# Hybrid decoder block on one core: sums on DVE alone, a ninth weight slot and an earlier spare tile, logits in one step, down bias moved

## The chip, the core and the metric

The kernel runs on one core of a Trainium2 chip. Its engines are PE (TensorE), DVE (VectorE), ACT (ScalarE), POOL (GpSimd) and SP (SyncE), which here only issues DMAs. The time is that of the device, in microseconds, for one execution.

## The reference

One layer for 256 tokens of width 1024, all in float32: a modulated norm, four token mixers that share one input projection, a gated merge, an output projection, and then a mixture of 32 experts of which each token uses four.

```python
mod = c_act @ w_ada[l] + b_ada[l]
shift1, scale1, gate1, shift2, scale2, gate2 = (m[:, None, :] for m in jnp.split(mod, 6, axis=-1))
h = rms_norm(x, g_norm_mix[l]) * (1.0 + scale1) + shift1
z = h @ w_in[l]                      # four mixers' inputs and the merge logits
...
up = jnp.einsum('bsnc,ncd->bsnd', ys, w_branch[l])
gates = jax.nn.sigmoid(merge_logits.reshape(B, S, N_BRANCHES, D))
x = x + gate1 * (jnp.sum(gates * up, axis=2) @ w_out[l])
h2 = rms_norm(x, g_norm_ffn[l]) * (1.0 + scale2) + shift2
# moe_ffn: logits = h2 @ w_router + b_router; top 4 of 32; softmax over them
for e in range(N_EXPERTS):
    gu = h @ w_gate_up[e] + b_gate_up[e]
    ...
    y = y + combine[:, e:e + 1] * (act @ w_down[e] + b_down[e])
return rms_norm(x + gate2 * y, g_final)
```

The weights of the experts are 192 tiles of 2 MiB (four `wg` and two `wd` for each expert), 403 MB; all of the kernel reads 468 MB.

## The kernel before

**Products in float32.** Each large product of the front is made from two halves of both operands: `split` (L335) lets ACT write the rounded high half (L347) and DVE the rest, source minus high half (L348), and PE then does three products (high by high, high by low, low by high). The split works on 512 columns at a time, in four rotating buffers each.

**The front, 0 to 307 us.** The six vectors of the modulation are sums over 8 blocks of rows of `w_ada`, each row block scaled by the conditioning. For four of them `ada` (L237) does this in halves of 512 columns, step by step in the background of other work: the first four blocks are scaled by ACT (L249; for one vector by POOL, L247) and added by POOL (L251), the other four scaled and added by DVE (L254); `ada_end` lets PE transpose and reduces the sum. The mixers' projections and the merge use `z_unit` (L364): four splits of 512, each followed by 12 matmuls and a step of the background work (`bg`, the mixers; `slow_step`, the sums). A merge unit, 16 in all (four branches by four column blocks), is one `z_unit`, a sigmoid on ACT, the branch's up-projection `pu` (L809, from two splits of 256), a multiplication by the gate on DVE (L816) and an addition into `mix`, on POOL for the second and third branch (L817). The output projection `pw` (L765) runs in the last branch's units; `out_split` (L768) first lets POOL multiply each 512 columns of `wo` by `gate1` (L774).

**The router, 307 to 320 us.** `x1_logits` transposes the new x and multiplies it with the router's weights in four strips of 32 rows, a copy of the result (L895) and a second product with a selecting matrix (L896) add the strips. DVE finds the top four, their mask and positions. The gather `pg` (L1000) picks the expert's tokens by a matmul with a 0/1 matrix `pm`.

**The experts.** 16 pairs. For a pair PE does gate-up (`ea`, `eb`, L1067; its bias is a small matmul, L1058), a transposition (`eat`, L1081) and down (`ed`, L1094) of the one expert and then of the other; `spread` (L1032) prepares from the combine weights, with products by POOL (L1024), the matrices by which `scatter` (`py`, L1104) adds the pair's rows to the tokens. `down_bias` (L959) adds the bias of the down projections of all experts at once: two transposes, four matmuls `pyb` (L970), eight DVE operations.

**What sets the order.** A scheduler places each engine's instructions by the program's order and dependences; `tc.issue_after` holds an instruction behind another. Expert tiles go through a ring: `load_wide` (L134) takes the next slot and issues the load on SP, whose queue works in order, so that a load that waits for its slot holds all that follow. There are 5 slots (`RING`, used as 1 MiB halves in the front) and 3 more (`EXTRA`) from the third merge branch on, when the mixers' buffers are closed. Eight tiles are loaded into them during the output projection. A spare tile (`sp`, the first expert's fourth) uses space that the front gives back. In the program the bias rows `bgu` (L953, four loads on SP) stand ahead of it, in a buffer that is free after the router's mask.

## Time and profile before

| | |
|---|---|
| median of 3 runs | 1263.29 us (1259.78 to 1267.72) |
| profiled execution | 1264.25 us, span 1262.5 us |
| PE busy | 1172.2 us (93%) |
| DVE busy | 484.4 us (38%) |
| ACT busy | 204.8 us (16%) |
| POOL busy | 131.2 us (10%) |
| read from HBM | 467.81 MB |
| mean granted clock | 0.991 |

The shares are means over stages with different limits. The chain of waits says what released the last work at each step; the windows show which engine is full in a stage and at which rate the DMA runs; the waits of SP show when a load stood for its slot, and the waits of PE when PE stood for a load. A busy PE is not PE at its peak, since the ends of matmuls are modelled.

### The profile page before, as it was taken

What the parts mean: (1) busy time and instruction counts of PE and PEld (TensorE: products, weight loads), DVE (VectorE), ACT (ScalarE), POOL (GpSimd) and SP (SyncE); (2) the same over time, 40 slices, a digit from 0 to 9 for tenths busy, and PEclk for the clock granted to TensorE, in tenths of its full rate; (3) what the DMA queues carried; (4) which work ended last, traced back from release to release, by engine and by line L of the source; (5) the groups of instructions that cost most, each with busy time, mean ns of one, the idle gap of its engine ahead of it and who ended that gap; (6) DMA issues with size and microseconds to landing.
All of it is one profiled execution on the core that took longest, in us unless ns stands there. A gap on an engine that the chain in (4) does not pass through costs nothing.

```text
span 1262.5 us, 14878 instructions
## 1 busy us (share of the span) xinstructions
PE 1172.2 (93%) x6204; PEld 567.7 (45%) x6204; DVE 484.4 (38%) x833; ACT 204.8 (16%) x403; POOL 131.2 (10%) x171
## 2 busy tenths in 40 slices
PE   7999999989999999999999999999989998989875
PEld 4778798987333433333333333333323332332224
DVE  3797598986342312222222223222212222132123
ACT  3458355445100000000000000000000000000001
POOL 2332213740000000000000000000000000000001
PEclk9999899999999999999999999999999999999999
DMA  9975369947889999999999999999999999999994
GB/s 324 337 248 201 133 221 341 346 160 276 320 365 396 429 427 429 427 427 428 428 428 428 428 428 428 426 428 427 429 427 428 427 428 428 428 427 428 427 382 145
DMA packets 74730, 469.88 MB, mean 372 GB/s; under 512 B 6425, under 2 KB 27010, under 8 KB 50594
## 3 DMA queue, kind: packets, MB, share of 16 engines
q1 hardware_dynamic: 74034, 467.64, 90.6%
q10 hardware_dynamic: 624, 1.23, 0.3%
q8 instruction: 50, 0.82, 0.3%
q14 instruction: 22, 0.18, 0.0%
HBM read 467.81 MB, written 1.05 MB: 371 GB/s over the span
## 4 chain that ended last, share of the span: by engine, by line
PE 61%; DMA 23%; DVE 10%; issue 2%; ACT 1%; POOL 1%; ACTq 0%; SPq 0%; POOLq 0%; DVEq 0%
DMA wd<-in_w_down_dram 13%; PE ed L1094 13%; PE ea L1067 12%; PE eb L1067 12%; DMA wg<-in_w_gate_up_dram 9%; PE pz_m L361 5%; PE py L1104 4%; PE pg L1000 2%; PE pw L765 2%; PE pu L809 1%; PE pdl L1128 1%; DMA wada<-in_w_ada_dram 1%; PE eat L1081 1%; DVE el L1045 1%; DVE el L1047 1%
## 5 line engine op out<-in xcount | busy, mean ns | idle before, releaser
L1067 PE MATMUL ea<-wg,he 128*64 128x512 f32 x1024 | 284.9, 600 | 8.9 <-DMA wg<-in_w_gate_up_dram 8.7
L1067 PE MATMUL eb<-wg,he 128*64 128x512 f32 x1024 | 283.6, 593 | 0.0
L1094 PE MATMUL ed<-wd,aT 128*64 128x512 f32 x960 | 214.6, 598 | 9.5 <-DMA wd<-in_w_down_dram 8.3
L1041 DVE TENSOR_SCALAR eg<-ea 128x512 f32<-128x512 f32 x32 | 22.1, 692 | 356.6 <-PE ea L1067 352.5
L1043 ACT ACTIVATE es<-eg 128x512 f32<-128x512 f32 x32 | 20.2, 630 | 827.9 <-DVE eg L1041 827.9
L1067 PEld LDWEIGHTS eb<-wg,he 128*64 128x64 f32 x1024 | 80.2, 137 | 146.9 <-issue 146.8
L1067 PEld LDWEIGHTS ea<-wg,he 128*64 128x64 f32 x1024 | 72.9, 137 | 145.6 <-issue 119.4
L1094 PEld LDWEIGHTS ed<-wd,aT 128*64 128x64 f32 x960 | 67.4, 137 | 143.8 <-issue 126.9
L1024 POOL TENSOR_TENSOR pc<-pm,comb 128x128 f32<-128x128 f32 x64 | 23.5, 402 | 685.2 <-PE psm L1032 624.3
L361 PE MATMUL pz_m<-hh,wl_m 128*128 128x256 f32 x256 | 73.3, 286 | 5.9 <-DVE wl_m L348 5.8
L361 PE MATMUL pz_m<-hh,wh_m 128*128 128x256 f32 x256 | 73.6, 287 | 0.0
L361 PE MATMUL pz_m<-hl,wh_m 128*128 128x256 f32 x256 | 72.1, 282 | 0.0
L1106 DVE TENSOR_TENSOR x_sb<-x_sb,py 128x512 f32<-128x512 f32 x60 | 41.3, 688 | 30.3 <-PE py L1104 30.3
L361 PEld LDWEIGHTS pz_m<-hh,wl_m 128*128 128x128 f32 x256 | 49.0, 191 | 8.0 <-DVE wl_m L348 7.7
L1104 PE MATMUL py<-oa,sm 128*128 128x512 f32 x60 | 33.8, 645 | 19.4 <-DVE oa L1098 19.4
L361 PEld LDWEIGHTS pz_m<-hl,wh_m 128*128 128x128 f32 x256 | 49.1, 192 | 0.1
L361 PEld LDWEIGHTS pz_m<-hh,wh_m 128*128 128x128 f32 x256 | 49.0, 191 | 0.3
L1097 DVE TENSOR_TENSOR oa<-ed,late 64x512 f32<-64x512 f32 x15 | 10.2, 683 | 94.6 <-PE ed L1094 94.6
L1097 DVE TENSOR_TENSOR ob<-ed,late 64x512 f32<-64x512 f32 x15 | 10.2, 682 | 91.0 <-PE ed L1094 91.0
L348 DVE TENSOR_TENSOR wl_m<-win_m,wh_m 128x512 fp32r<-128x512 f32 x44 | 42.0, 971 | 7.0 <-ACT wh_m L347 6.9
L1058 PE MATMUL ea<-bgu,ident 32*64 32x512 f32 x128 | 36.5, 612 | 0.0
L1081 PEld LDWEIGHTS eat<-ident,el 128*128 128x128 f32 x128 | 17.6, 205 | 41.0 <-DVE el L1047 39.3
(450 smaller groups left out, 1567.8 us busy)
## 6 DMA issues: line engine op xcount, KB each, us to landing
wg<-in_w_gate_up_dram SPq DMA_DIRECT2D x128, 2048.0 KB, 26.7
wd<-in_w_down_dram SPq DMA_DIRECT2D x60, 2048.0 KB, 27.0
wada<-in_w_ada_dram SPq DMA_DIRECT2D x13, 1024.0 KB, 7.4
win_m<-in_w_in_dram SPq DMA_DIRECT2D x11, 1024.0 KB
win_c<-in_w_in_dram SPq DMA_DIRECT2D x8, 1024.0 KB, 8.2
wada<-in_w_ada_dram SPq DMA_DIRECT2D x12, 512.0 KB, 7.3
wl<-in_w_down_dram SPq DMA_DIRECT2D x5, 1024.0 KB, 28.8
wada<-in_w_in_dram SPq DMA_DIRECT2D x4, 1024.0 KB, 8.1
```

The lines of the kernel that those rows point to most:

```text
L348: V.tensor_tensor(lk, sk, f32(wk), ALU.subtract)
L361: T.matmul(pz[:, b * 256:(b + 1) * 256], l, r, start=(kh == 0 and b == 0 and kk == 0 and i == 0), stop=last and i == 2, skip_group_check=True)
L765: T.matmul(pw[t, hf_], m_[:, kk, t * P:(t + 1) * P], w[:, 0, :], start=(k == 0 and i == 0), stop=(k == KC - 1 and i == 2))
L1000: last_i["pg"] = T.matmul(pg[:, kk * 256:(kk + 1) * 256], chan(n2[:, t, :], k), pm[:, t].rearrange("p e s -> p (e s)"), start=(i == 0), st ...
L1024: G.tensor_tensor(pc[:, t, :, var, i ^ var, :], pv_[:, :, i, :], cv[:, :, i].unsqueeze(2).to_broadcast([P, EB // 2, CAP]), ALU.mult)
L1041: V.tensor_scalar(g, pa, 7.0, None, ALU.min)
L1058: T.matmul(pp_[64 * j:64 * j + 64, :], ident[r:r + NE, r + e:r + e + 1].to_broadcast([NE, CAP]), bgu[r:r + NE, :], start=True, stop=False, ...
L1067: T.matmul(pp_[64 * j:64 * j + 64, :], he[:, k, (e % EB) * CAP:(e % EB + 1) * CAP], w[:, i * DE + j * 512:i * DE + (j + 1) * 512], start=F ...
L1081: T.transpose(pt[:, q * P:(q + 1) * P], cols, ident)
L1094: T.matmul(pd[64 * jj:64 * jj + 64, :], aT[:, k % 4, 64 * (k // 4):64 * (k // 4) + 64], w[k % 4][:, o * 512:(o + 1) * 512], start=(k == 0) ...
L1104: T.matmul(py, s_[:, hf_, t * P:(t + 1) * P], o, start=True, stop=True)
L1106: V.tensor_tensor(yv, yv, py, ALU.add)
```

## The change

Seven things, in the order of the program.

1. The sums of the modulation (`ada`) are done for all 1024 columns at once by DVE alone, eight operations per vector; ACT and POOL no longer take part.
2. `split` works on 1024 columns: a `z_unit` does two splits instead of four, a branch unit one of 512 instead of two of 256, a row block of `wo` one instead of two. There are three rotating buffers of 1024 instead of four of 512.
3. The small subtraction L403 and the additions into `mix` are DVE's. `wo` is no longer multiplied by `gate1`; instead `out_last` multiplies each finished 512 columns of the projection by it before x is added.
4. The router's product gives the logits of 128 tokens directly, in eight accumulating matmuls; the copies and the selecting product go. The chain after it runs per token tile.
5. `bgu` is loaded on ACT's queue into a buffer of its own when the mixers close. Behind the eight tiles SP so finds the spare tile, which now waits for the last multiplication of the projection, and then a ninth tile, in a slot that joins the ring there.
6. `spread` and the first pair's `scatter` come after the gate-up of expert 2.
7. `down_bias` is done in four quarters behind the scatters of experts 8, 10, 12 and 14.

The core of the diff:

```diff
-WP = 4
+WP = 3
...
-    def ada(s_, j):
...
+    def ada(s_, i):
+        w = load_rows(f"wada{s_}_{i}", w_ada[0, i * 512:(i + 1) * 512, s_ * D:(s_ + 1) * D], D)
...
         def run():
-            for k in range(4):
-                if s_ == 2:
-                    G.tensor_tensor(w[k], w[k], cact[:, k:k + 1].to_broadcast([P, 512]), ALU.mult)
+            for kk in range(4):
+                k = 4 * i + kk
+                if k == 0:
+                    V.tensor_scalar(acc, w[kk], cact[:, k:k + 1], None, ALU.mult)
                 else:
-                    A.activation(w[k], w[k], AF.Copy, scale=cact[:, k:k + 1])
-                if k:
-                    G.tensor_tensor(w[0], w[0], w[k], ALU.add)
+                    V.scalar_tensor_tensor(acc, w[kk], cact[:, k:k + 1], acc, ALU.mult, ALU.add)
                 yield
-            for k in range(4, KC):
-                V.scalar_tensor_tensor(acc, w[k], cact[:, k:k + 1], w[0] if k == 4 else acc, ALU.mult, ALU.add)
-                yield
...
-        for k in range(nk if sw else 1):
-            wk, lk, sk = [t[:, k] for t in (wh, wl, src)] if sw else (wh, wl, src)
-            A.activation(wk, sk, AF.Copy)
-            V.tensor_tensor(lk, sk, f32(wk), ALU.subtract)
-        return ws
+            A.activation(wh, src, AF.Copy)
+            V.tensor_tensor(wl, src, f32(wh), ALU.subtract)
+        return wh, wl
...
     def z_unit(tiles, c0, name, token, sw=False):
         pz = bank("z", f"pz_{name}")
-        for kh in range(4):
-            wh, wl = split(tiles[kh // 2][:, 2 * (kh % 2):2 * (kh % 2) + 2, c0:c0 + 256], 2, 256, f"{name}_{kh}", sw)
-            z_part(pz, wh, wl, kh, token)
-            bg()
-            slow_step()
+        for i in range(2):
+            wh, wl = split(tiles[i][:, :, c0:c0 + 256], 4, 256, f"{name}_{i}", sw)
+            for j in range(2):
+                z_part(pz, wh[:, 2 * j:2 * j + 2, :], wl[:, 2 * j:2 * j + 2, :], 2 * i + j, token)
+                bg()
+                slow_step()
...
-            (G if kk else V).tensor_tensor(hl[:, k, :], hf, f32(hh[:, k, :]), ALU.subtract)
+            V.tensor_tensor(hl[:, k, :], hf, f32(hh[:, k, :]), ALU.subtract)
...
-            for w in (wo[k], wo[k + 1]):
-                for h in range(2):
-                    c = slice(h * 512, (h + 1) * 512)
-                    G.tensor_tensor(w[:, c], w[:, c], gate1[:, c], ALU.mult)
...
+            bgu = lb.tile([P, 512], F32, tag="bgu", name="bgu")
+            for j in range(4):
+                A.dma_start(bgu[NE * j:NE * j + NE, :], b_gate_up[0, :, j * 512:(j + 1) * 512])
...
-                (V if bi == 3 else G).tensor_tensor(mv, mv, sg, ALU.add)
+                V.tensor_tensor(mv, mv, sg, ALU.add)
...
-        V.tensor_tensor(x_sb[:, t, cs], x_sb[:, t, cs], pw[t, g], ALU.add)
+        tm = mp.tile([P, 512], F32, tag="t2", name=f"gx{t}{g}")
+        V.tensor_tensor(tm, pw[t, g], gate1[:, cs], ALU.mult)
+        V.tensor_tensor(x_sb[:, t, cs], x_sb[:, t, cs], tm, ALU.add)
...
-            T.matmul(pls[t][32 * kk:32 * kk + 32, 0:P], wr2[:, 4 * g + kk, :], xt[:, kk, :], start=(g == 0),
-                     stop=(g == 1))
...
+            pl_i[t] = T.matmul(pls[t][:, 0:NE], xt[:, kk, :], wr2[:, k, :], start=(k == 0), stop=(k == KC - 1)).ins
...
-        V.tensor_copy(lT[:, t, :], pls[t][:, 0:P])
-        sel_i = T.matmul(pls[t][:, P:P + NE], lT[:, t, :], id4, start=True, stop=True, skip_group_check=True).ins
...
+    add_slots(ctx.enter_context(tc.tile_pool(name="r9", bufs=1, side="right")), 1)
     with tc.tile_pool(name="sp", bufs=1, side="right") as sp:
         u = wg_src(0, 3)
         pref[u[0]] = load_wide(*u, pool=sp)
-        gate_up_bias(0, (sel_i, sel_i))
+        u = units[RING + EXTRA]
+        pref[u[0]] = load_wide(*u)
+        gate_up_bias(0, (pl_i[1], pl_i[1]))
...
             a0 = gate_up(e, he)
+            if late_sc:
+                sm = spread(b, pm)
+                scatter(0, sm[0], *late_sc.pop())
...
-                down_bias()
-            if sm is None:
+            elif sm is None:
                 sm = spread(b, pm)
             down(e + 1, a1, oa, ob)
+            if e == 0:
+                late_sc.append((oa, ob))
+                continue
             scatter(e, sm[r], oa, ob)
+            if 8 <= e < 16:
+                down_bias(e // 2 - 4)
```

What this does to the order on the engines, at three places.

SP's queue behind the first tiles, before (`wg_3_3563` is a tile of the second expert, `wd_0_3565` the eighth tile, `wg_3_3710` the spare):

```order
L136 DMA wg_3_3563<-in_w_gate_up_dram 128x4096
L136 DMA wd_0_3565<-in_w_down_dram 128x4096
L953 DMA bgu<-in_b_gate_up_dram 32x512 x4
L136 DMA wg_3_3710<-in_w_gate_up_dram 128x4096
L136 DMA wd_1_3889<-in_w_down_dram 128x4096
L136 DMA wd_0_3969<-in_w_down_dram 128x4096
```

and now (`wg_3_3310` is the spare, `wd_1_3312` the tile in the ninth slot):

```order
L134 DMA wg_3_3166<-in_w_gate_up_dram 128x4096
L134 DMA wd_0_3168<-in_w_down_dram 128x4096
L134 DMA wg_3_3310<-in_w_gate_up_dram 128x4096
L134 DMA wd_1_3312<-in_w_down_dram 128x4096
L134 DMA wd_0_3522<-in_w_down_dram 128x4096
L134 DMA wd_1_3532<-in_w_down_dram 128x4096
```

The four bias loads have left the queue; the spare and the ninth tile follow the eighth, and the load `wd_0_3522` is the first behind them that waits for a slot that an expert used.

PE at the router, before (`pnt` are the transposes of x, `pl` the router's products, `pb` the rows of the last gate, `ppos` the positions from the mask):

```order
L865 MATMUL pnt_3619<-ident,x_sb 128x128 x4
L865 MATMUL pnt_3631<-ident,x_sb 128x128 x4
L873 MATMUL pl_3528<-x1T_3624,wr_1632 32x128 x4
L873 MATMUL pl_3529<-x1T_3636,wr_1632 32x128 x4
L896 MATMUL pl_3528<-sel 128x32
L896 MATMUL pl_3529<-sel 128x32
L294 MATMUL pb_0_3653<-ident,modT 128x128 x4
L294 MATMUL pb_1_3654<-ident,modT 128x128 x4
L911 LDWEIGHTS ustr
L911 MATMUL ppos<-mask,ustr 128x32
L912 LDWEIGHTS oneb
L912 MATMUL ppos<-mask,oneb 128x32
```

and now:

```order
L857 MATMUL pnt_3239<-ident,x_sb 128x128
L867 MATMUL pl_3144<-wr_1514,scr 128x32 x4
L857 MATMUL pnt_3239<-ident,x_sb 128x128 x3
L912 LDWEIGHTS ustr
L912 MATMUL ppos<-mask,ustr 128x32
L913 LDWEIGHTS oneb
L913 MATMUL ppos<-mask,oneb 128x32
L867 MATMUL pl_3144<-wr_1514,scr 128x32 x4
L289 MATMUL pb_0_3252<-ident,modT 128x128 x4
L289 MATMUL pb_1_3253<-ident,modT 128x128 x4
L914 LDWEIGHTS ustr
L914 MATMUL ppos<-mask,ustr 128x32
```

The two selecting products are gone; the first token tile's `ppos` stands ahead of the second's last products.

PE at the first two experts' down projections, before (`ed_3880` of the first expert stands ahead of this piece; `ed_3968` is the second's):

```order
L963 MATMUL pct<-ident,comb 32x128 x2
L1094 MATMUL ed_3968<-wd_0_3969,aT_3876 64x512
L970 MATMUL pyb_3925<-bdn,cT 128x512
L970 MATMUL pyb_3930<-bdn,cT 128x512
L970 MATMUL pyb_3935<-bdn,cT 128x512
L1094 MATMUL ed_3968<-wd_0_3969,aT_3876 64x512 x2
L970 MATMUL pyb_3940<-bdn,cT 128x512
L1094 MATMUL ed_3968<-wd_0_3969,aT_3876 64x512 x2
L1032 MATMUL psm_0_3955<-ident,pc_3945 128x128 x4
L1094 MATMUL ed_3968<-wd_0_3969,aT_3876 64x512 x2
L1032 MATMUL psm_1_3962<-ident,pc_3945 128x128 x4
L1094 MATMUL ed_3968<-wd_0_3969,aT_3876 64x512
```

and now (`ed_3483` is the first expert's, `ed_3521` the second's):

```order
L1092 MATMUL ed_3483<-wd_0_3168,aT_3426 64x512 x8
L1092 MATMUL ed_3483<-wd_1_3312,aT_3426 64x512 x8
L939 LDWEIGHTS oneb
L939 MATMUL pcnt<-mask,oneb 128x32
L939 LDWEIGHTS oneb
L939 MATMUL pcnt<-mask,oneb 128x32
L1065 MATMUL ea_3544<-wg_0_3550,he_3330 64x512
L1065 MATMUL eb_3545<-wg_0_3550,he_3330 64x512 x2
L1065 MATMUL ea_3544<-wg_0_3550,he_3330 64x512
L1092 MATMUL ed_3521<-wd_0_3522,aT_3479 64x512 x8
L1092 MATMUL ed_3521<-wd_1_3532,aT_3479 64x512 x8
L1065 MATMUL ea_3544<-wg_0_3550,he_3330 64x512
```

The transposes and matmuls of the down bias and the eight of the spread no longer stand between them; four matmuls of the third expert's gate-up do.

## Rows read from the trace of the kernel before

**Rows 1.** The page: rates in 40 slices of the span; the chain's shares by engine.

```profile
GB/s 324 337 248 201 133 221 341 346 160 276 320 365 396 429 427 429 427 427 428 428 428 428 428 428 428 426 428 427 429 427 428 427 428 428 428 427 428 427 382 145
...
PE 61%; DMA 23%; DVE 10%; issue 2%; ACT 1%; POOL 1%; ACTq 0%; SPq 0%; POOLq 0%; DVEq 0%
```

**Rows 2.** Windows, one stretch of experts: busy us (count) per engine, PE clock, DMA share, GB/s.

```profile
800.00:840.00 40.00, 37.98 (x169) 12.56 (x165) 8.87 (x13) 0.63 (x1) 0.00 (x0) 1.00 1.01 427
```

**Rows 3.** Windows by stage of the front, the same columns.

```profile
50.00:100.00 50.00, 47.48 (x335) 40.15 (x335) 48.97 (x106) 31.25 (x83) 19.37 (x15) 1.00 0.72 252
...
173.00:268.00 95.00, 88.19 (x722) 85.66 (x720) 90.04 (x116) 48.64 (x92) 53.19 (x33) 0.98 0.84 314
268.00:302.00 34.00, 33.68 (x210) 30.37 (x210) 23.65 (x42) 18.35 (x32) 0.00 (x0) 1.00 0.56 223
```

**Rows 4.** Chain of waits in order of time, 173 to 281 us: start, length (us), what.

```profile
173.08 1.44 PE pu L809 x12
...
217.29 1.78 PE pb L294 x16
...
268.37 1.10 PE pu L809 x7
...
274.98 5.65 PE pz_m L361 x48
```

**Rows 5.** Durations by source: ns min/median/max, first and last start (us), shapes.

```profile
L254 DVE SCALAR_TENSOR_TENSOR acs<-wada,cact,acs x24: 737/750/1786, 73.5 to 233.0; 128x512 f32<-128x512 f32 x24
...
L348 DVE TENSOR_TENSOR wl_m<-win_m,wh_m x44: 677/690/1775, 135.1 to 288.2; 128x512 fp32r<-128x512 f32 x44
L348 DVE TENSOR_TENSOR wl_b<-wb,wh_b x16: 411/418/1517, 145.7 to 246.3; 128x256 fp32r<-128x256 f32 x16
```

**Rows 6.** Groups of DVE instructions, 173 to 268 us: busy us, mean ns | idle before.

```profile
L348 DVE TENSOR_TENSOR wl_m<-win_m,wh_m 128x512 fp32r<-128x512 f32 x34 | 35.2, 1054 | 1.9 <-ACT wh_m L347 1.8
L254 DVE SCALAR_TENSOR_TENSOR acs<-wada,cact,acs 128x512 f32<-128x512 f32 x12 | 12.9, 1073 | 0.1
L348 DVE TENSOR_TENSOR wl_b<-wb,wh_b 128x256 fp32r<-128x256 f32 x10 | 7.9, 802 | 0.5 <-ACT wh_b L347 0.5
```

**Rows 7.** Timeline of SP's DMA issues: start, length (us), line, what.

```profile
302.80 0.33 SPq L136 DMA_DIRECT2D wd<-in_w_down_dram  x1
313.27 1.72 SPq L953 DMA_DIRECT2D bgu<-in_b_gate_up_dram  x4
315.04 0.54 SPq L136 DMA_DIRECT2D wg<-in_w_gate_up_dram  x1
323.39 3.76 SPq L136 DMA_DIRECT2D wd<-in_w_down_dram  x2
...
379.48 3.76 SPq L136 DMA_DIRECT2D wg<-in_w_gate_up_dram  x2
```

**Rows 8.** Timeline of DVE in the router, the same columns.

```profile
310.49 0.29 DVE L895 COPY sel<-pl 128x128 f32<-128x128 f32 x1
```

**Rows 9.** Timeline of PE in the router, the same columns.

```profile
310.35 0.89 PE L896 MATMUL pl<-sel 128*128 128x32 f32 x4
...
316.76 1.07 PE L1058 MATMUL ea<-bgu,ident 32*64 32x512 f32 x4
```

**Rows 10.** SP's waits, 302 to 386 us: total us, times, longest us.

```profile
SPq L953 <- DVE mask L909: 10.0, 1, 10.0
```

**Rows 11.** Windows of 10 us around the two holes, columns as in the second group.

```profile
310.00:320.00 10.00, 8.59 (x61) 5.89 (x63) 8.88 (x30) 4.92 (x11) 2.15 (x3) 1.00 0.51 166
...
370.00:380.00 10.00, 8.43 (x30) 2.70 (x28) 5.32 (x9) 0.00 (x0) 4.25 (x11) 0.83 0.42 180
```

**Rows 12.** PE's waits, 330 to 1262 us: total us, times, longest us.

```profile
PE ea L1067 <- DMA wg<-in_w_gate_up_dram: 8.7, 10, 1.3
PE ed L1094 <- DMA wd<-in_w_down_dram: 8.3, 8, 1.2
```

**Rows 13.** ACT's high-half copies, 40 to 305 us: busy us, mean ns | idle before.

```profile
L347 ACT ACTIVATE wh_m<-win_m 128x512 fp32r<-128x512 f32 x44 | 26.2, 627 | 26.5 <-PE pz_rg L361 11.9 <-PE pz_m L361 7.1 <-PE pu L809 3.0
```

More of the change, by code (lines that the diff above doesn't have):

```diff
@@ L770, in out_split @@
             wo[k], wo[k + 1] = load_rows(f"wo{k}", w_out[0, k * P:(k + 2) * P, :], 1024)
-            for w in (wo[k], wo[k + 1]):
-                for h in range(2):
-                    c = slice(h * 512, (h + 1) * 512)
-                    G.tensor_tensor(w[:, c], w[:, c], gate1[:, c], ALU.mult)
-        cs = slice(hf_ * 512, (hf_ + 1) * 512)
-        held[k, hf_] = split(wo[k][:, cs].unsqueeze(1), 1, 512, f"o{k}{hf_}")
+        if hf_ == 0:
+            wh, wl = split(wo[k].rearrange("p (h f) -> p h f", h=2), 2, 512, f"o{k}")
+            for h in range(2):
+                held[k, h] = wh[:, h:h + 1, :], wl[:, h:h + 1, :]
     mixs = {}
@@ L801, in hybrid_block_kernel @@
             A.activation(sg, pz, AF.Sigmoid)
-            wsp = [split(wb[k][:, u * 256:(u + 1) * 256].unsqueeze(1), 1, 256, f"b{n}_{u}{k}") for k in range(2)]
+            wbh, wbl = split(wb[:, :, u * 256:(u + 1) * 256], 2, 256, f"b{n}_{u}")
             pu = bank("t", f"pu{n}_{u}")
@@ L900, in hybrid_block_kernel @@
         rss.append(ssq2[:, t, 3:4])
-    with tc.issue_after(sel_i):
-        pb5 = gate_rows(5, "ab")
-    for t in range(NT):
-        V.scalar_tensor_tensor(lg[:, t, :], pls[t][:, P:P + NE], rss[t], brt, ALU.mult, ALU.add)
+        n2_first(t)
+        V.scalar_tensor_tensor(lg[:, t, :], pls[t][:, 0:NE], rss[t], brt, ALU.mult, ALU.add)
         V.max(mx[:, t, :], lg[:, t, :])
@@ L913, in hybrid_block_kernel @@
     pp_i = T.matmul(pp[:, NE:2 * NE], ustr, mask[:, 1, :], start=False, stop=True, skip_group_check=True).ins
+    with tc.issue_after(mask_i):
+        n2_low(0, slice(0, 256))
     V.scalar_tensor_tensor(pos, pp[:, 0:NT * NE].rearrange("p (t e) -> p t e", t=NT), 1.0, mask, ALU.add, ALU.mult)
-    for q in range(4):
+    for q in range(1, 4):
         for t in range(NT):
@@ L919, in hybrid_block_kernel @@
                 A.activation(n2h[:, t, cs], x_sb[:, t, cs], AF.Copy, scale=rss[t])
-    for t in range(NT):
-        with tc.issue_after(sq_i[NT - 1, 1]):
-            A.activation(scr[:, t, 0:256], x_sb[:, t, 0:256], AF.Copy, scale=rss[t])
-        G.tensor_tensor(n2l[:, t, 0:256], scr[:, t, 0:256], f32(n2h[:, t, 0:256]), ALU.subtract)
     def combine():
@@ L950, in hybrid_block_kernel @@
     comb = epa.tile([P, NT, NE], F32, tag="comb", name="comb")
-    bgu = epa.tile([P, 512], F32, tag="bgu", name="bgu")
-    for j in range(4):
-        nc.sync.dma_start(bgu[NE * j:NE * j + NE, :], b_gate_up[0, :, j * 512:(j + 1) * 512])
-    bdn = epa.tile([NE, D], F32, tag="pc", name="bdn")
+    bdn = epa.tile([NE, D], F32, tag="bdn", name="bdn")
     A.dma_start(bdn, b_down[0])
@@ L985, in gather @@
             last_i["pm"] = pm_i.ins
+            with tc.issue_after(pm_i.ins):
+                n2_low(1, slice(0, 256))
             for q in range(1, 4):
```

163 lines of the change are left out of this document (82 added, 81 removed).

## The prediction

> **What bounds the kernel now.** I read the page's chain of waits first. By engine it is PE with a DMA share [rows 1]: no single engine to shorten, so the stages must be taken apart. The line of DMA rates [rows 1] cuts them: below 400 GB/s and uneven in the first thirteen slices (to about 410 us), flat at 425 to 429 from there to 1200 us, and falling off in the last two. One stretch of the flat part [rows 2] shows the DMA share at 1.01 with PE busy 37.98 of 40 us: the experts run at the pace of the weight stream, 2 MiB (2.097 MB) per 4.90 us at 428 GB/s, with PE close behind. So two things move the end: how early the stream reaches its full rate, and how many of its 192 tiles lie in SBUF by then. The work on either side of that moment only matters through these.
>
> In the front (0 to 307 us) the stage windows [rows 3] show DVE busy 48.97 of 50 and 90.04 of 95 us with POOL working beside it, and 23.65 of 34 us with POOL idle. The chain there alternates PE groups with DVE's low halves: from the end of one merge unit's last PE group at 173.1 to the same point at 268.4 lie 11 units in 95.3 us [rows 4], while in the stretch with POOL idle a unit's own matmuls take 5.65 + 1.44 = 7.09 us [rows 4]. The durations by source say why DVE is full: the same 512-wide subtraction takes 690 ns in the median and up to 1775, the same multiply-add 750 and up to 1786 [rows 5]; over 173 to 268 us, with POOL at work, their means are 1054 and 1073 [rows 6]. One instruction at one size with a fast median and a mean half as long again is held up by something in part of its runs.
>
> **The change part by part.**
>
> *Front, DVE and POOL.* Every POOL operation on whole tiles goes from the front; DVE gains the mix adds and wider sums and loses the halved instructions. No row before is a 1024-wide subtraction. Bounds: below, one 512-wide 0.69; above, two of them, 1.38. I take the width slope: 418 ns at 256, 690 at 512 [rows 5], so 0.272 per 256 more, 1.23 us at 1024. For 173 to 268 us: 44 subtractions cost about 45 us before, 22 x 1.23 = 27 after; 22 branch halves at 0.80 [rows 6] 17.6 before, 11 x 0.69 = 7.6 after; 16 sums of 512 were about 16 us, 16 of 1024 at 1.23 are 20; mix adds +7 x 0.69 = 4.8; the 11 us of other work stay. DVE falls from 90 to about 71 us. Then PE sets the pace: 11 x 7.09 = 78, plus two groups of 16 matmuls for gate and router rows, 1.78 for the one [rows 4], plus (an estimate from the same per-matmul time) some 5.5 for the sums' transposes and the mixers' rest: 87 us. Gain 95.3 - 87 = 8. Bounds 2 to 14 (14 is 95.3 - 81.5, the units and those two groups alone). For 50 to 173 us DVE is as full, but the mixers' chains across PE, ACT and DVE stand there too; half as much, 4 (0 to 8). At the start the low half of h leaves POOL: I put 1 (0 to 2) for it. Front: **13 us**, bounds 2 to 22. Dropping the 16 multiplications of wo by the gate costs DVE four of 0.69 at the projection's end; three lie beside PE's matmuls, the fourth is in the next term. ACT loses 24 copies and gains the four bias loads, which POOL's and SP's queues no longer see; ACT has slack there, so I cost them at nothing, 1.72 us, what they took on SP, if that cover is gone [rows 7].
>
> *Logits in one step.* DVE's copy of 0.29 [rows 8] and PE's select matmuls, 0.89 for both token tiles with the wait between [rows 9], go; on the path of the second token tile I count 0.85 us. The last copy of the transposed x is cut in two (-0.3); the fourth gate multiplication is added (+0.65). The first expert's bias matmuls, 1.07 us for each of two banks [rows 9], stood between the gather's groups and now stand ahead of them while PE waits; but DVE's gather copies there wait behind six small subtractions, now seven (+0.4), so 1.3 of their 2.1 us come through. PE now stands at the first token tile's mask with the second's last four logits matmuls queued behind it; I take that mask to be done beside the second's last transposes and copy, and if it is late the term loses up to 1 us. Together **2 us**, bounds 0 to 3.
>
> *Stream after the front.* Before, SP issued the eighth tile at 302.80, then sat in front of the bias loads until the router's mask (10.0 us [rows 10]) and issued them at 313.27, the spare tile at 315.04, the next at 323.39 [rows 7]; 310 to 320 us ran at 166 GB/s [rows 11]. Now the spare waits only for DVE's last gate multiplication at the end of the projection, and the ninth slot's tile stands directly behind it with nothing of its own to wait for. The eighth tile was still on its way then, so both follow it without a hole. The following tile waits, as before, for PE's last matmul on the first expert's first tile. Everything later on SP is queued behind this wait, one tile further ahead than it was. The price: one more tile of 2 MiB in SBUF before a wait that stays where it is, **4.9 us**, bounds 0 (PE cannot use it) and 4.9.
> The Trainium skill (DMA: Bandwidth & Descriptors, Specifications) gives 358 GB/s as the limit of a core's HBM reads, by which the tile would be worth 5.9 us and the sum 1 us more; the 426 to 429 GB/s of this trace say otherwise, and I go by them.
>
> *Down bias and first scatter.* Before, four bias matmuls, two transposes and eight spread matmuls, which wait for POOL's products, stood between the first two down projections; the load into the slot of the second's first tile went out at 379.48 us [rows 7], and 370 to 380 us ran at 180 GB/s [rows 11]. At 428 GB/s that window lacks 5.8 us, and by the issue and its start-up the next one some 1.4: a hole of about 7.2 us. Now the second follows the first at once, spread and scatter come after the third gate-up, the bias work behind the scatters of experts 8 to 14, where DVE is busy 8.87 of 40 us [rows 2]; PE's work stays the same in sum. **7.2 us**, bounds 3 (the slot comes free earlier, but the later stall of the same kind stays) and 7.2.
>
> *Sum.* 13 + 2 + 4.9 + 7.2 = 27.1. The profiled execution took 1264.25 (span 1262.5): 1237.2. The median of the three runs is 0.96 lower: **1236 us**. The tail after the last load stays as it is. PE must have room for the stream's 12 us: its waits for DMA after 330 us are 8.7 + 8.3 = 17.0 [rows 12], so 5 remain. It is enough, but thin.
>
> **The rivals.**
>
> *1. The front gives little.* ACT's wider copies, mixers and PE hold it once DVE is relieved; front 3 instead of 13: 1246. For: PE is busy 88.19 of 95 us [rows 3]. Against: PE's own floor above. Chance 0.20.
>
> *2. DVE's long instructions are not POOL's doing.* Then the moved work comes on top: in 173 to 268 us the 16 wide sums at 1.7 instead of 1.0 add 11, the mix adds at 0.96 add 7, the merged splits save little; 50 to 173 us adds half of that. Front 13 longer with 14 won behind it: 1262, no change. Against: the two levels [rows 5]. Chance 0.05.
> The Trainium skill (Perfetto Trace Analysis, Optimizing Scalar/DVE Operations) advises to offload work from a saturated DVE to the other engines, the reverse of this change, and by it the time would be that 1262; the same section warns that DVE and GpSimd share a port, and the trace, 690 against 1775 ns, is with the warning.
>
> *3. PE becomes the bound of the experts.* If PE's room is half of 12 us, the rest of the stream's gain ends as holes at its far end: 1242. For: the 5 us left. Chance 0.13.
>
> *4. Slower: the wide splits are exposed.* A half unit now waits for one ACT copy of 1024 and one subtraction of 1024 where 512 of each did. ACT took 627 ns at 512 [rows 13], so between that and 1.25 at 1024; with the same relative slope as DVE's about 1.05: 2.28 against 1.32 us, 0.96 more for each of 48 halves, with three buffers instead of four. If no split can be made ahead, 46 us: from 1236 + 13, as the front then keeps none of its gain, to 1295. It turns slower than before from 15 of the 48, and by over 1% from 28. Against: ACT is half idle, so it can run one half ahead, and a half's matmuls take 2.8 us. Chance 0.07.
>
> That the change does not do what it says, the spare still issued late, could show only if SP were held by an older tile; it would give 5 of the 14.1 back: inside the range.
>
> **How the numbers follow.** The forecast has 0.55. A measurement tells about 1% (12.6 us) from no change: faster is below 1250.7, slower above 1275.9. Faster: 0.55, 0.13 and 0.15 of the first rival's 0.20, 0.83. Same: its other 0.05, the second's 0.05, some 0.01 of the fourth: 0.11. Slower: 0.06. The range runs from 1223 (all upper bounds together give 37 and 1226, and the fastest run of before lies 3.5 under its median) to 1250 (the first rival with most of the ninth slot unpaid).
>
> **What would show it.** Right: in the front no DVE subtraction of one shape over twice its median; DVE below 80% where it had 95%; projection's end near 294 us instead of 307; no hole in the DMA rate between the eighth and tenth tile, nor 40 us later; from there 428 GB/s to the end. Wrong: PE waiting for the high or low halves in most units (rival 4), subtractions of 1024 over 1.7 us (rival 2), or holes in the stream after 700 us (rival 3).

## The result and the profile after

The changed kernel takes **1230.13 us** (median of 4 runs, 1229.39 to 1231.55) against 1262.19 for the kernel before in the same comparison (4 runs, 1259.78 to 1267.72): a ratio of 0.9741, 95% interval 0.9707 to 0.9775. The forecast was 1236, range 1223 to 1250. The profiled execution took 1229.39 us with a span of 1227.7, 34.8 us less than the span before; the accounting below is in spans.

The page after: busy time by engine, rates in 40 slices of the span, and the chain's shares.

```profile
PE 1154.9 (94%) x6200; PEld 562.1 (46%) x6200; DVE 451.8 (37%) x762; ACT 177.6 (14%) x297; POOL 41.4 (3%) x109
...
GB/s 321 342 271 230 182 258 394 344 204 334 364 427 427 429 428 427 427 427 428 430 426 428 427 428 430 427 426 428 427 428 429 427 428 428 428 427 430 428 372 145
...
PE 69%; DMA 19%; DVE 8%; ACT 1%; issue 1%; POOL 0%; ACTq 0%; SPq 0%; POOLq 0%; DVEq 0%
```

The flat part of the rates begins at the twelfth slice, where [rows 1] had it at the fourteenth, and is no higher. The chain has gone from DMA to PE (23% to 19%, 61% to 69%).

Windows after, columns as in [rows 2]: three stretches of the front, the eleven units of the merge that the prediction counts (161.83 to 246.36 us), and three windows behind the front.

```profile
50.00:100.00 50.00, 49.86 (x356) 42.41 (x357) 39.58 (x91) 29.85 (x70) 0.00 (x0) 1.00 0.74 276
173.00:250.00 77.00, 76.56 (x650) 75.35 (x649) 63.50 (x79) 32.24 (x41) 0.00 (x0) 1.00 0.95 364
132.00:136.00 4.00, 4.00 (x33) 2.84 (x33) 2.12 (x4) 0.00 (x0) 0.00 (x0) 1.00 0.06 22
...
161.83:246.36 84.53, 84.09 (x723) 83.07 (x721) 72.06 (x94) 35.05 (x45) 0.00 (x0) 1.00 0.96 366
...
310.00:320.00 10.00, 10.00 (x47) 3.26 (x48) 3.87 (x7) 2.35 (x3) 0.00 (x0) 1.00 0.71 302
320.00:330.00 10.00, 10.00 (x48) 3.23 (x44) 0.42 (x1) 0.00 (x0) 0.00 (x0) 1.00 0.89 347
350.00:360.00 10.00, 10.00 (x50) 3.30 (x45) 0.61 (x1) 0.00 (x0) 0.00 (x0) 1.00 1.02 433
```

Beside [rows 3], DVE has gone from 98% to 79% of the window 50 to 100 and from 95% to 85% of the eleven units, and PE now fills both, 99.4% of 173 to 250. The last row lies where the second pair of experts starts and shows no hole; [rows 11] had 180 GB/s at that place of the program.

The chain of waits after, columns as in [rows 4]: the last PE group of the unit whose group stood around 268.37 there, and one unit's 48 matmuls.

```profile
246.52 1.42 PE pu L804 x12
253.41 5.65 PE pz_m L354 x48
```

By the start of the last matmul of these groups in the timelines, the eleven units go from 163.1 to 247.7 us now and went from 174.2 to 269.2 before: 84.5 us where they took 95.0. (The 95.3 of the prediction runs from the second matmul of one group to the sixth of the other.) A unit's own matmuls are as long as before, 5.65 us.

Durations by source after: the 1024-wide subtraction and sum.

```profile
L341 DVE TENSOR_TENSOR wl_m<-win_m,wh_m x22: 1214/1226/1244, 125.5 to 264.4; 128x1024 fp32r<-128x1024 f32 x22
L245 DVE SCALAR_TENSOR_TENSOR acs<-wada,cact,acs x23: 1265/1281/1301, 67.1 to 215.0; 128x1024 f32<-128x1024 f32 x23
```

No subtraction is over 1.5% above its median, where [rows 5] had 1775 over 690.

SP's issues after, in the order of [rows 7], and its wait there.

```profile
278.19 0.33 SPq L134 DMA_DIRECT2D wd<-in_w_down_dram  x1
286.32 0.33 SPq L134 DMA_DIRECT2D wg<-in_w_gate_up_dram  x1
286.70 17.73 SPq L134 DMA_DIRECT2D wd<-in_w_down_dram  x3
308.85 37.25 SPq L134 DMA_DIRECT2D wg<-in_w_gate_up_dram  x8
...
SPq L134 <- DVE gx L849: 7.8, 1, 7.8
```

The eighth tile goes out at 278.19, the spare at 286.32 after 7.8 us of waiting for the last gate multiplication, the ninth slot's at 286.70.

PE in the router after: the projection's last matmul, two groups of the logits, and the first expert's start.

```profile
285.04 0.48 PE L758 MATMUL pw<-wh_o,ml 128*128 128x512 f32 x1
...
286.68 1.08 PE L867 MATMUL pl<-wr,scr 128*128 128x32 f32 x8 [0.21 <-ACT scr L864]
...
287.77 0.98 PE L867 MATMUL pl<-wr,scr 128*128 128x32 f32 x8
...
296.98 1.08 PE L1065 MATMUL ea<-wg,he 128*64 128x512 f32 x4 [0.25 <-DVE he L1008]
```

Before, the same last matmul stood at 307.28 and the first `ea` 12.41 us behind it; now it is 11.94.

PE's waits: after, for the loads from 320 us on and for the subtraction in the whole front; then before, in the front.

```profile
PE ed L1092 <- DMA wd<-in_w_down_dram: 6.4, 6, 1.2
PE ea L1065 <- DMA wg<-in_w_gate_up_dram: 5.3, 6, 1.2
...
PE pz_m L354 <- DVE wl_m L341: 1.2, 2, 0.8
```

```profile
PE pz_m L361 <- DVE wl_m L348: 5.8, 6, 1.7
PE pu L809 <- DVE wl_b L348: 2.5, 4, 1.0
PE po_gla L667 <- DVE glat L654: 2.1, 2, 1.6
```

**Where the 34.8 us come from.** The end of the projection (that last matmul) is 307.28 - 285.04 = 22.2 us earlier. Of these, 1.9 lie ahead of the first matmul of `pz_sq` (57.2 before, 55.3 now) and 20.3 behind it. In the eight profiles that have the changed kernel's front (this one and those of the router and stream experiments below, control included) this first part ends anywhere from 54.0 to 56.2 us, while the rest of the front takes 229.2 to 229.9; so the 20.3 are firm and the 1.9 are not. The router gives 0.5. What is left, 12.1, lies between the first `ea` and the end.

The stream shows where. A hole is here a stretch in which the bytes moved, summed from the DMA packets of the trace, fall behind 428 GB/s, and its size is the time lost. Before there were 1.3 us (303 to 306), 6.8 (309 to 320), 1.9 (323 to 327), 4.9 (340 to 346) and 7.1 (374 to 383). Now there are 0.9 (279 to 282), 2.7 (285 to 289), 0.5 (294 to 297), 2.2 (300 to 304) and 4.8 (317 to 323): 11.1 in sum against 22.0. The hole of 7.1 is gone; the first is mostly filled.

### The profile page after: what moved, and what is told of

Same layout as the page of the kernel before. It is cut to its first block, busy times and chain, and to the rows that moved or that the text cites. A ratio compares the mean times of both kernels' runs of the same rounds, so it can differ in the third digit from the quotient of the medians.

```text
span 1227.7 us, 14486 instructions
## 1 busy us (share of the span) xinstructions
PE 1154.9 (94%) x6200; PEld 562.1 (46%) x6200; DVE 451.8 (37%) x762; ACT 177.6 (14%) x297; POOL 41.4 (3%) x109
## 4 chain that ended last, share of the span: by engine, by line
PE 69%; DMA 19%; DVE 8%; ACT 1%; issue 1%; POOL 0%; ACTq 0%; SPq 0%; POOLq 0%; DVEq 0%
PE ea L1065 14%; PE eb L1065 13%; PE ed L1092 13%; DMA wd<-in_w_down_dram 12%; DMA wg<-in_w_gate_up_dram 6%; PE pz_m L354 6%; PE py L1102 4%; PE pw L758 2%; PE pg L998 2%; PE pu L804 1%; PE pdl L1126 1%; PE eat L1079 1%; DVE el L1043 1%; DVE el L1045 1%; DVE es L1044 1%
## 5 line engine op out<-in xcount | busy, mean ns | idle before, releaser
L1065 PE MATMUL ea<-wg,he 128*64 128x512 f32 x1024 | 280.0, 600 | 5.7 <-DMA wg<-in_w_gate_up_dram 5.3
L1065 PE MATMUL eb<-wg,he 128*64 128x512 f32 x1024 | 278.2, 594 | 0.0
L1092 PE MATMUL ed<-wd,aT 128*64 128x512 f32 x960 | 211.5, 595 | 7.5 <-DMA wd<-in_w_down_dram 6.4
L1065 PEld LDWEIGHTS ea<-wg,he 128*64 128x64 f32 x1024 | 72.1, 137 | 142.6 <-issue 123.7
L1095 DVE TENSOR_TENSOR oa<-ed,late 64x512 f32<-64x512 f32 x15 | 10.2, 682 | 94.6 <-PE ed L1092 94.6
L1095 DVE TENSOR_TENSOR ob<-ed,late 64x512 f32<-64x512 f32 x15 | 10.2, 682 | 89.7 <-PE ed L1092 89.7
L1056 PE MATMUL eb<-bgu,ident 32*64 32x512 f32 x128 | 36.5, 612 | 0.0
```

Source lines behind the costliest of these rows:

```text
L1056: T.matmul(pp_[64 * j:64 * j + 64, :], ident[r:r + NE, r + e:r + e + 1].to_broadcast([NE, CAP]), bgu[r:r + NE, :], start=True, stop=False, ...
L1065: T.matmul(pp_[64 * j:64 * j + 64, :], he[:, k, (e % EB) * CAP:(e % EB + 1) * CAP], w[:, i * DE + j * 512:i * DE + (j + 1) * 512], start=F ...
L1092: T.matmul(pd[64 * jj:64 * jj + 64, :], aT[:, k % 4, 64 * (k // 4):64 * (k // 4) + 64], w[k % 4][:, o * 512:(o + 1) * 512], start=(k == 0) ...
L1095: V.tensor_tensor(lo[0:64, :], pd[0:64, :], gate2[0:64, sw * 512:(sw + 1) * 512], ALU.mult)
```

## The experiments

Each kernel is the changed one with the edit shown. Times are medians of four or five runs; the changed kernel itself ran once more as control, and its median was 1230.13 again.

**The changed kernel again.** 

> The changed kernel once more, beside the others on the same chip, as the measure for them: 1230 within 1.5 us.

Measured: 1230.13 (1229.39 to 1233.63), ratio 0.9768 [0.9747, 0.979]. So 1230.13 serves below for all kernels. The two ratios of the changed kernel, 0.9741 and 0.9768, differ by 0.0027, which is 3.4 us: differences below that between kernels not measured beside each other are not to be trusted.

### The front

**Useless work for POOL.** 56 doublings in place, of data that nobody reads again, where POOL worked before.

```diff
+    def noise(t):
+        G.tensor_tensor(t, t, t, ALU.add)
...
+                noise(w[kk][:, 0:512])           # after each sum
...
+                if bi < 3:
+                    noise(sg)                    # after each mix add
...
+                noise(wo[k][:, h * 512:(h + 1) * 512])
```

> The changed kernel, with POOL operations put back beside it that compute nothing that is used: each doubles in place 512 columns of a tile that DVE and ACT are done with (32 in the sums, 8 in the merge units, 16 on the rows of wo), the number and places of before. DVE's and ACT's own work is that of the changed kernel. Theory A (POOL's operations hold DVE's up): DVE's 1024-wide operations of 1.22 to 1.28 us show maxima over 2 us, POOL is busy some 80 us, and the front ends 6 to 20 us later: 1236 to 1250. Theory B (what pays is the merging, or ACT's relief): one duration as now, and 1230 within 3 us.

Measured: 1246.65, +16.5 us; ratio to before 0.9878 [0.9859, 0.9898]. The end of the projection is 16.1 later. Durations by source in this kernel, columns as in [rows 5], and PE's wait for the subtraction:

```profile
L345 DVE TENSOR_TENSOR wl_m<-win_m,wh_m x22: 1208/1226/2059, 126.9 to 277.2; 128x1024 fp32r<-128x1024 f32 x22
L248 DVE SCALAR_TENSOR_TENSOR acs<-wada,cact,acs x23: 1272/1462/2059, 67.2 to 226.2; 128x1024 f32<-128x1024 f32 x23
...
PE pz_m L358 <- DVE wl_m L345: 7.6, 7, 2.0
```

DVE and PE have the same work as in the changed kernel; only POOL has more. The longest subtraction goes from 1244 to 2059 ns, and PE's wait for it from 1.2 to 7.6 us. So POOL's work beside DVE costs DVE time, whatever it is for. One rival remains: the doublings also keep the weights' buffers longer, and loads start later. SP waits for POOL 35.9 us in sum in this front, and ACT once 7.3 us for a load. But no wait of PE between 40 us and the end of the projection is for a load or for that copy, so the loss does not come from there.

**The sums back on ACT and POOL alone** (the old `ada`), **the mix adds and the gate multiplication of `wo` back on POOL alone**, and **both**.

```diff
-    def ada(s_, i):        # eight DVE operations of 1024
+    def ada(s_, j):        # the old one: halves, ACT and POOL first
```

> The changed kernel with the modulation's sums as before alone: halves of 512 columns, scaled by ACT (one vector by POOL), added by POOL, the other four blocks by DVE. Theory A (POOL's operations hold DVE's up, and a stand of PE at 127 to 130 us that this causes lowers PE's granted clock for the 10 us behind it): DVE's maxima over 2 us again before 230 us, the stand or one like it comes back, and the front ends 8 to 14 us later: 1238 to 1244. Theory B (DVE alone is as slow, since it now does all eight blocks): within 3 us of 1230.

```diff
-                V.tensor_tensor(mv, mv, sg, ALU.add)
+                (V if bi == 3 else G).tensor_tensor(mv, mv, sg, ALU.add)
...
+                    G.tensor_tensor(w[:, c], w[:, c], gate1[:, c], ALU.mult)
...
-        V.tensor_tensor(tm, pw[t, g], gate1[:, cs], ALU.mult)
```

> The changed kernel with the mix adds of two branches and the multiplication of wo by the gate back on POOL (and so no gate multiplications at the projection's end on DVE). Theory A (POOL holds DVE up where both work): subtractions over 2 us between 180 and 270 us, the front 4 to 9 us later, less 0.7 us for the shorter chain at its end: 1234 to 1239. Theory B (the share of POOL's work in this stretch is hidden): 1229 to 1231.

> The changed kernel with both the sums and the mix adds and gate multiplications back on POOL; the splits stay 1024 wide. Singly these cost the front 8.7 and 5.5 us. Theory A (each is held up in its own stretch): the front 14 us later and about 1245. Theory B (the two meet on the same DVE, which then is the bound of the whole merge stretch): 17 to 20 us later, 1247 to 1250, so that with the 2.7 us of the narrow splits the front's 22 us are accounted for.

Measured: sums 1238.41 (+8.3; ratio 0.9807 [0.9781, 0.9832]), mix adds and gate 1237.11 (+7.0; 0.9785 [0.9761, 0.9808]), both 1249.26 (+19.1; 0.9912 [0.9887, 0.9938]). The ends of the projection are 8.7, 5.5 and 18.5 us later. Counted from the first matmul of `pz_sq`, the front takes 229.7 us in the changed kernel, 250.1 before and 248.5 with both back on POOL: these two moves hold 18.8 of the 20.3 us. The same window (columns as in [rows 2]) of the three kernels, in this order, and for the last PE's wait for the subtraction from 133 to 305 us:

```profile
173.00:250.00 77.00, 73.53 (x618) 72.94 (x617) 62.65 (x75) 36.88 (x51) 14.84 (x9) 0.98 0.95 361
```

```profile
173.00:250.00 77.00, 73.53 (x633) 72.59 (x632) 68.09 (x67) 28.85 (x38) 44.16 (x23) 1.00 0.92 352
```

```profile
173.00:250.00 77.00, 69.33 (x558) 68.51 (x556) 63.80 (x64) 34.45 (x47) 38.33 (x24) 0.93 0.96 358
...
PE pz_m L357 <- DVE wl_m L344: 7.7, 4, 3.1
```

PE is idle 3.5 of 77 us with either and 7.7 with both, so the idle times about add; the granted clock is 0.98 and 1.00 with either but 0.93 with both, and 77 times the missing 0.05 is 3.9 us. That is the size of the surplus, 19.1 - 8.3 - 7.0 = 3.8. I read it so: PE's stands (its waits with nothing to do) are paid twice, once as idle time and once in the clock. This is argued from one profiled execution of each, not shown. With the sums alone PE stood 1.9 us up to 180.9 and the clock fell behind it; with the mix adds alone it stood 2.2 us up to 220.1 and the clock stayed at 1.00, so not every stand is paid twice. Theory B of the last expectation has the time right, but not its reason: DVE is busy 63.80 of the 77 us with both, where it was 62.65 with the sums alone.

**Narrow splits in the same buffers.**

```diff
-            A.activation(wh, src, AF.Copy)
-            V.tensor_tensor(wl, src, f32(wh), ALU.subtract)
+            for h in range(2):
+                ks = slice(h * nk // 2, (h + 1) * nk // 2)
+                A.activation(wh[:, ks], src[:, ks], AF.Copy)
+                V.tensor_tensor(wl[:, ks], src[:, ks], f32(wh[:, ks]), ALU.subtract)
```

> The changed kernel, with each split of up to 1024 columns done as two ACT copies and two DVE subtractions of half the width, in the same three buffers; POOL stays out of the front. Theory A (the front's 22 us come from DVE and ACT no longer sharing the sums with POOL, so that no DVE operation is held up): DVE does two times 0.69 instead of 1.23 us, 0.15 more for each split, which PE's pace in the units hides; subtractions stay at one duration near 690 ns; time within 5 us of the changed kernel's 1230. Theory B (the merging of instructions pays): the front falls back by 10 us or more, 1240 to 1252. Theory C (the wide splits cost something, since PE has to wait for the whole of them): a few us faster than 1230.

Measured: 1233.75, +3.6; ratio 0.9784 [0.9757, 0.981]. Durations by source of the 512-wide subtraction in this kernel:

```profile
L343 DVE TENSOR_TENSOR wl_m<-win_m,wh_m x44: 681/685/694, 128.7 to 267.6; 128x512 fp32r<-128x512 f32 x44
```

The shape that took up to 1775 ns in [rows 5] has one duration here, with POOL out of the front. The projection ends 2.7 later, but all of that lies ahead of the first matmul of `pz_sq` (58.0 against 55.3 us); from there both kernels take 229.7 us to the projection's end. So the wide splits are not a hidden loss in the units, and narrow ones cost nothing there; nor do they fill up the front's 22 us, as the last expectation has it. Whether the 2.7 at the start belong to them is open: 58.0 is one execution, and the other eight lie between 54.0 and 56.2.

### The router

**The four strips and the selecting product back.**

```diff
-            T.matmul(pls[t][:, 0:NE], xt[:, kk, :], wr2[:, k, :], start=(k == 0), stop=(k == KC - 1))
+            T.matmul(pls[t][32 * kk:32 * kk + 32, 0:P], wr2[:, k, :], xt[:, kk, :], start=(g == 0), stop=(g == 1))
...
+        V.tensor_copy(lT[:, t, :], pls[t][:, 0:P])
+        T.matmul(pls[t][:, P:P + NE], lT[:, t, :], id4, start=True, stop=True)
```

> The changed kernel with the router's product as before: four strips of 32 rows (weights of 32 columns on the stationary side), a copy and a selecting product for each token tile; the rest of the chain stays per token tile. In the changed kernel's trace the logits in one step stand at 1.0 us for each half tile where the strips took 0.43, and the new term gave 0.5 instead of 2 us. Theory A (the one-step product costs PE as much as the strips and the selection saved): the first expert starts within 1 us of the changed kernel's distance of 11.4 us behind the last projection matmul, or up to 1.5 us earlier; 1228.5 to 1230.5. Theory B (the forecast's: the one step saves 0.85 us of chain): 1 to 2 us later, 1231 to 1232.

Measured: 1230.34 (+0.2; ratio 0.9735 [0.9713, 0.9756]); from the projection's last matmul to the first `ea` 11.98 us against 11.94. PE's weight loads for the logits, first of the changed kernel, then of this one (form, count, busy us, mean ns):

```profile
L867 PEld LDWEIGHTS pl<-wr,scr 128*128 128x128 f32 x32 | 3.9, 193 | 0.6 <-ACT scr L864 0.6
```

```profile
L871 PEld LDWEIGHTS pl<-scr,wr 128*32 128x32 f32 x32 | 0.8, 108 | 1.8 <-ACT scr L868 0.8 <-DVE scr L866 0.5 <-ACT scr L865 0.4
```

Logits in one step make the transposed x, 128 columns, the stationary operand in place of 32 columns of the router's weights. Each half of a token tile so takes PE about 1.0 us instead of 0.42 (0.43 in this kernel's rows). The strips' kernel spends that time elsewhere: in its timeline PE waits 0.33 and 0.22 us for the copies ahead of the last strips and 0.40 ahead of the selecting product. In sum the two forms are equal.

### The stream

**Without the ninth slot; with the down bias, spread and first scatter back; with both.**

```diff
-    add_slots(ctx.enter_context(tc.tile_pool(name="r9", bufs=1, side="right")), 1)
...
-        u = units[RING + EXTRA]
-        pref[u[0]] = load_wide(*u)
```

> The changed kernel without the ninth slot (the spare tile stays where it is). Forecast of the sum: the slot is worth one tile of 2 MiB, 4.9 us: 1235. Rival (PE is the bound of the experts, the slot is not used): 1230 to 1231.

```diff
-            if late_sc:
-                sm = spread(b, pm)
-                scatter(0, sm[0], *late_sc.pop())
...
-            elif sm is None:
+                for i in range(4):
+                    down_bias(i)
+            if sm is None:
                 sm = spread(b, pm)
...
-            if 8 <= e < 16:
-                down_bias(e // 2 - 4)
```

> The changed kernel with the down bias, the spread and the first scatter back between the first two down projections. Forecast of the sum: the hole of 7.2 us in the stream comes back some 60 us after the router: 1237. Rival (the ninth slot or PE hides it): 1230 to 1233.

> The changed kernel without the ninth slot and with the down bias, the spread and the first scatter back between the first two down projections: only the front, the router and the earlier spare tile are left of the change. Theory A (the two gains in the stream are holes of their own, and add up): 1230 + 5.6 + 6.3 = 1242. Rival (one hole hides the other, or PE does): 1236 to 1239.

Measured: 1235.76 (+5.6; ratio 0.9792 [0.9771, 0.9813]), 1236.45 (+6.3; 0.9798 [0.9777, 0.9818]) and 1241.38 (+11.3; 0.985 [0.9825, 0.9875]). (In the second and third the down bias also writes to another buffer, `eg` for `oa`.) One window of the first kernel (columns as in [rows 2]), then one of the second:

```profile
300.00:310.00 10.00, 10.00 (x49) 3.71 (x46) 1.69 (x8) 1.18 (x3) 2.90 (x8) 1.00 0.74 279
```

```profile
350.00:360.00 10.00, 10.00 (x34) 3.14 (x34) 3.61 (x6) 0.00 (x0) 2.90 (x8) 0.72 0.46 159
```

Without the ninth slot the stream is at 279 GB/s here, and has a hole of 7.9 us (294 to 305) at the tenth tile, where the changed kernel loses 2.7 in its two small ones. With the down bias back it is at 159 GB/s where the changed kernel has 433, with a hole of 6.6 us (353 to 361) at the twentieth tile. The two add up (5.6 + 6.3 = 11.9 against 11.3, each within some 3 us), so PE followed the stream for both gains together.

**The next hole.** Of the changed kernel's holes the largest left, 4.8 us, stands at the fourteenth tile, whose slot PE frees late. Three tiles of the second expert's gate-up ahead of the first expert's fourth:

```diff
     def first(k2, he):
+        if k2 == 3:
+            gate_up_bias(1, (last_i["pg"], last_i["pg"]))
+            for k in range(6):
+                gate_up_part(1, he, k)
```

> A version that goes on from the changed kernel: PE does three tiles of the second expert before the first expert's fourth tile, which lies in the spare buffer and so gives no slot of the ring back. In the changed kernel the stream stands 4.6 us at the 14th tile because that slot comes free one tile later. Theory A (the stream's start still sets the end): that hole falls to 1 to 2 us and the time to about 1227. Theory B (PE is the bound, or the hole moves): 1229.5 to 1231.

Measured: 1229.51, 0.6 less than the control; ratio 0.9726 [0.9704, 0.9747]: no difference that can be told. The hole at the fourteenth tile went, but the one at the eleventh grew from 2.2 to 5.2 us (301 to 308), 2.3 came at 340 to 344, and the router took 14.6 us instead of 11.9. In sum the stream loses 11.5 us from 278 to 360, as in the changed kernel (11.3). A window of the router's second half, columns as before:

```profile
292.00:298.00 6.00, 6.00 (x29) 4.29 (x29) 3.57 (x13) 1.67 (x5) 0.00 (x0) 0.53 0.98 381
```

The granted clock was 0.53 there; the changed kernel has 1.00 in this window in its own profile. The order need not be the cause: in the control, which is the changed kernel itself, the clock was 0.80 over 290 to 296 and the router took 13.6 us. What the order is worth where PE keeps its clock was still open, so I ran the two edits together, the strips of the router and this order:

```diff
+            T.matmul(pls[t][32 * kk:32 * kk + 32, 0:P], wr2[:, k, :], xt[:, kk, :], start=(g == 0), stop=(g == 1))
...
+        if k2 == 3:
+            for k in range(6):
+                gate_up_part(1, he, k)
```

> A version that goes on: the strips and selection of e6 and the order of e9 together. In e9 the hole at the 14th tile was gone, but PE's granted clock was 0.53 over 6 us of the router, which took 2.6 us back. Theory A (the order is worth the hole where PE keeps its clock): about 1227 with a clock of 1.00 between 284 and 300 us. Rival (the lost time only moves, to a hole at a later tile): 1229 to 1231 with the clock at 1.00.

Measured: **1228.05** (1226.34 to 1228.85), 2.1 less than the control, whose lowest run of 1229.39 is above its highest; ratio 0.9743 [0.9724, 0.9763] against the control's 0.9768, measured beside it.

Three of its windows, columns as before:

```profile
290.00:296.00 6.00, 5.65 (x46) 4.66 (x47) 5.54 (x18) 1.73 (x5) 0.00 (x0) 1.00 1.01 393
310.00:320.00 10.00, 10.00 (x50) 3.36 (x48) 0.56 (x2) 1.78 (x2) 0.00 (x0) 1.00 1.00 427
...
330.00:340.00 10.00, 10.00 (x47) 3.53 (x46) 2.63 (x5) 0.00 (x0) 0.00 (x0) 1.00 0.86 333
```

The window 310 to 320 is at 427 GB/s where the changed kernel had 302, and the clock did not fall in this execution. But part of the hole only moved, as the rival said: 330 to 340 has 333 GB/s where the changed kernel has 431, and 2.2 of the 4.8 us come back there (336 to 341). The stream loses 8.4 us from 278 to 360 instead of 11.3, which fits the 2.1 measured. This is the version to go on with, small as its lead is. That it is better than the order alone is not shown: that kernel's ratio was 0.9726, against another set of runs of before.

## Why the prediction was right, and where it was not

**The front: right mechanism, size too small** (13 forecast, 22.2 measured, just over the upper bound of 22). What was said of DVE and POOL held: the 1024-wide subtraction was put at 1.23 us and takes 1.226; one duration instead of two levels; useless work for POOL alone puts the projection's end back by 16.1 us of the 22.2. What the prediction did not have is the clock. The term that failed is "half as much, 4" for 50 to 173 us, with 1 for the start. The lead of the changed kernel is 1.9 us at the first matmul of `pz_sq` (55.3 against 57.2), 3.5 at the first matmul of `pz_rg` (120.2 against 123.7), 10.2 at its last (129.6 against 139.8), and 11.1 at the third merge unit: 11.1 instead of 5. The jump of 6.7 lies within `pz_rg`, and rows of the kernel before, which the prediction does not use, show it (three additions of POOL and one of the subtractions beside them, from the timelines; then two windows, columns as in [rows 2]):

```profile
122.84 5.06 POOL L251 TENSOR_TENSOR win_m<-win_m 128x512 f32<-128x512 f32 x3 [12.48 <-ACT win_m L249]
...
124.99 1.77 DVE L348 TENSOR_TENSOR wl_rg<-win_c,wh_rg 128x512 fp32r<-128x512 f32 x1
...
128.00:132.00 4.00, 2.21 (x7) 1.31 (x8) 2.88 (x7) 0.00 (x0) 0.00 (x0) 0.75 0.59 180
132.00:136.00 4.00, 4.00 (x18) 3.02 (x18) 0.89 (x2) 0.63 (x1) 0.00 (x0) 0.50 1.05 398
```

PE stood there for DVE's `glat` (2.1 us, the waits above), which was behind three operations of 512 that took 1.44, 1.77 and 1.37 us; the granted clock then fell to 0.50, the lower of the two levels, from 130 to 140 us. So in this execution one stand of 2.1 us cost three times its length. It is not this execution alone: the mean granted clock is 0.987 to 0.995 over 25 runs of the kernel before and 0.993 to 0.996 over 9 of the changed one. In the changed kernel the row 132 to 136 above has 33 matmuls where this one has 18, at full clock. With the sums back on ACT and POOL part of it returns, in that kernel's windows:

```profile
124.00:128.00 4.00, 2.38 (x13) 1.51 (x13) 2.52 (x5) 0.98 (x1) 0.65 (x1) 0.82 1.05 399
128.00:132.00 4.00, 4.00 (x24) 3.11 (x23) 1.17 (x2) 0.00 (x0) 0.00 (x0) 0.75 1.05 402
```

PE waits 1.6 us for `glat`, the clock is 0.82 and 0.75, and `pz_rg` takes 12.8 us from first to last start instead of 9.4. The page's line of the clock had shown the dip, as an 8 in the fifth slice among nines; I read the clock in windows of other stages only.

The other term, 8 for 173 to 268 us, was near: by the lead at the last unit (21.5) it is 10.4. Eleven units take 84.5 us where PE's floor was put at 87, and DVE is busy 72.1 us of them where 71 were forecast; PE does set the pace. The sign "DVE below 80%" came only for 50 to 100 us (79%): the units show 85%, and the prediction's own 71 of 87 us would have been 82.

**The router: wrong in size** (2 forecast, 0.5 measured). The step "DVE's copy and PE's select matmuls go" priced what was removed and not what the one step adds: weight loads of 193 instead of 108 ns, 32 of them. The strips' run shows the two forms as equal, 0.2 us apart. That explains 0.85 of the 1.5 us that are missing. PE also stood 0.35 us in front of the first token tile's `ppos`, which the prediction named as a risk; the rest is not broken down.

**The ninth slot and the down bias: right.** 4.9 and 7.2 were forecast; taken away, they cost 5.6 and 6.3, and the hole at the second expert went as a whole. That the spare and the ninth tile follow the eighth "without a hole" is nearly so: 2.7 and 0.5 us are lost there instead of 8.7 in the holes around the spare. The wait that "stays where it is" holds the eleventh tile until 300.67 and costs 2.2; the largest hole left, at the fourteenth tile, was not in the prediction.

**ACT's new loads and copies at nothing: right.** PE's waits for ACT's copies in the front are 1.6 us in sum, and were 1.1.

**The rivals.** 1, the front gives little: no, 22.2. 2, the long instructions are not POOL's: no, by the doublings. The Trainium skill (Perfetto Trace Analysis, Optimizing Scalar/DVE Operations) says that offloading from a saturated DVE may make sense, and in the same paragraph that between DVE and GpSimd it might not help, since they share a read port. These runs agree with the second: taking POOL's sums, mix adds and gate back to DVE paid 19.1 us. That the port is the reason no run here shows. 3, PE the bound of the experts: not reached. PE still waits 6.4 + 5.3 = 11.7 us for the loads after 320 us, where 17.0 - 12 = 5 was expected to be left. The stage from the first `ea` to the end, in windows before and after:

```profile
319.69:1262.50 942.81, 877.78 (x3998) 311.85 (x3996) 239.15 (x385) 43.34 (x77) 28.98 (x69) 0.99 0.98 410
```

```profile
296.98:1227.70 930.72, 872.71 (x3994) 312.09 (x3994) 240.08 (x387) 44.58 (x79) 29.38 (x69) 0.99 0.98 413
```

It is 12.1 us shorter, 7.0 of it from PE's idle time (65.0 to 58.0) and 5.1 from its busy time, with the same matmuls to do. The step "so 5 remain" took the waits alone for PE's room; the busy time, whose ends are modelled, held 5 us more. 4, wide splits exposed: no; PE waits for them 1.2 us in the front, and narrow ones are no faster.

The sum of spans came out as 22.2 + 0.5 + 12.1 = 34.8 against 27.1: 9.2 more in the front, most of it the 6.7 of the stand and its clock, and 1.5 less in the router. That the time came out 6 us under the forecast is therefore not to the prediction's credit; the terms that it priced from rows (8, 2, 4.9 and 7.2) came out within 3 us each.

## What to carry to other kernels

Where one DVE operation of one shape shows two levels of duration, look at what POOL does beside it before giving POOL more; here POOL's help with the sums, the mix adds and the gate cost more than it took over. Price a stand of PE with the clock that is granted behind it, so read the clock in windows of a few us and not by stage. A product that is made "in one step" changes which operand is loaded into PE: count those loads before calling the step shorter.
